# Half-array products of two heads issued in turn in every attention of a three-layer network

## The chip, the cores and the metric

One core of a Trainium2 chip runs the whole program. The metric is the device time of one execution in microseconds (us), the median of three. Between kernels, a difference of less than about 0.2% (3.7 us) can't be told from no change.

## What is computed

One sequence of 256 tokens, 1024 wide, goes through one block of a first kind and two layers of a second kind, all in float32. The parts that the change touches are the attentions:

```python
# first block: forgetting attention, 8 heads of 64, causal
sc = einsum('bqhd,bkhd->bhqk', qb, k) * scale + decay;  p = softmax(where(dist >= 0, sc, -inf))
o  = einsum('bhqk,bkhd->bqhd', p, v)
# first block: differential attention, 4 heads, two score maps (c = 0, 1) of 64 each, one value of 128
sc = einsum('bqhcd,bkhcd->bchqk', qb, k) * scale + bias;  w = p[:, 0] - lam * p[:, 1]
# both layers: window attention, 16 query heads of 64 on 4 key heads, |i - j| <= 128
# both layers: dilated attention, 12 sub-heads of 64 in 3 groups (dilation 1, 4, 16), 4 slots,
#              the groups of a slot mixed by their softmax denominators
```

Around them stand dense projections, a gated recurrence and a feed-forward part in the first block, and an expert-choice layer of 16 experts in each of the two layers, whose weights are most of the 562 MB that the program reads.

## The kernel before, in words

Activations stand transposed: features on the 128 partitions, the 256 tokens along the free axis. A dense product (`mm3`, lines 160 to 162) splits weight and activation into a high and a low part and issues three products of 128x128 by 256 columns. Weights come from memory through a ring of three 1 MB tiles, and ScalarE and VectorE split each (lines 154 and 155).

An attention head has 64 features, so two heads (or the two maps of a differential head), c = 0 and c = 1, share 128 partitions. Their **score products** take 64 rows of TensorE's array each (printed 64\*128 in the profile), their **value products** 64 columns each (128\*64), so each is a half-array product. They are plain float32, which the profile shows as two passes of each product.

- `scores` (line 405) is used by the forgetting and the differential attention: per pair of heads a 256-column and a 128-column product for each c.
- Line 460: value products of the forgetting attention, two per head.
- Line 877: value products of the window attention, two of 256 columns per head, eight pairs of heads in each layer. The first reads what ScalarE copied from the transposes of c = 0 (line 289), the second what it copied for c = 1.
- Lines 895 to 936: the dilated attention, written head by head. For each pair j, head c and query tile t there is one bank of scores: 256 columns by full-array products (lines 802 and 803), then two half-array products of 128 columns (line 908). VectorE reads the bank (line 910). After both query tiles of both heads come the value products, all of c = 0 and then all of c = 1 (lines 926 and 932).

Score tiles `ps_s` have two PSUM banks, value and transpose tiles `ps_v` and `ps_t` three together. The code isn't the order of issue: the framework plans it from its own timeline of each engine and fills TensorE with dense products of the projections while an attention waits for the other engines. Each engine then runs its own list strictly in that order, and waits on semaphores. The transposes (`to_T`, line 288) go between scores and values.

After a layer's attentions follow its gates, branch and output projections, and then the experts, whose weights (`we`) are loaded ahead into whatever buffers are free, paced by the projections (`Experts.pace`, `prefetch`).

Of the kernel before, what the change touches and what calls it, by code (L numbers as in the profile page):

```python
# [10 lines left out]
F32 = mybir.dt.float32  # L11
# [69 lines left out]
def tile_net(ctx: ExitStack, tc: tile.TileContext, a, out):  # L81
# [43 lines left out]

    def cols(t, c, n):
        return t[:, c : c + n]

    def pairs(ps):
        return ps.rearrange("p (n t) -> p n t", n=2)  # L130
# [176 lines left out]
    def first_block():  # L307
        with ExitStack() as es:
# [12 lines left out]
            def pss():  # L321
                return pp.tile([P, 512], F32, name="ps_s", tag="s", bufs=2)
# [73 lines left out]
            with tc.tile_pool(name="b1t", bufs=2, side="right", reuse_waits="tile") as tp:  # L396
# [2 lines left out]

                def scores(qs, ks, kt):  # L400
                    pq = [pss(), pss()]
                    for qr, kr, o in ((slice(128, 256), slice(0, 256), 0), (slice(0, 128), slice(0, 128), 256)):
                        for c in range(2):
                            b = slice(64 * c, 64 * c + 64)
                            nc.tensor.matmul(  # L405
                                pq[c][:, o : o + kr.stop], qs[b, kt, qr], ks[b, kt, kr], start=True, stop=True
                            )
                    return pq
# [20 lines left out]
                for j in range(4):  # L429
                    z = tp.tile([P, 2, 384], F32, name="z", tag="z")  # L430
                    pq = scores(fq, fk, j)

                    cm = tp.tile([P, 2, 384], F32, name="cm", tag="cm")
                    o = nck_d[2 * j : 2 * j + 2]
                    for lo, n in ((0, 256), (256, 128)):
                        nc.sync.dma_start(
                            cm[:, :, lo : lo + n],
                            bass.AP(tensor=o.tensor, offset=o.offset, ap=[[0, P], [T, 2], [1, n]]),
                        )
                    for c in range(2):  # L440
                        ends = cm[:, c, 128:384].rearrange("p (b k) -> p b k", b=2)
                        nc.gpsimd.tensor_tensor(
                            ends, ends, one("cmask").unsqueeze(1).to_broadcast([P, 2, P]), op=ALU.add
                        )
                        nc.vector.scalar_tensor_tensor(
                            z[:, c, :], pq[c][:, :384], 0.125, cm[:, c], op0=ALU.mult, op1=ALU.add
                        )
                    rs = soft(z)
                    pts = []
                    for c in range(2):  # L450
                        for t, s in SEG:
                            nc.vector.tensor_scalar(z[:, c, s], z[:, c, s], rs[:, t, c : c + 1], None, op0=ALU.mult)
                        pt = tp.tile([P, 384], F32, name="pt", tag="pt")
                        to_T(blocks(z[:, c]), pp, pt)
                        pts.append(pt)
                    po = psv()
                    for k, qr, pr in ((0, slice(0, 256), slice(0, 256)), (1, slice(128, 256), slice(256, 384))):
                        for c in range(2):
                            hv = slice((2 * j + c) * 64, (2 * j + c) * 64 + 64)
                            nc.tensor.matmul(  # L460
                                po[64 * c : 64 * c + 64, qr], fv[:, k, hv], pts[c][:, pr], start=k == 0, stop=k == 1
                            )
                    split_act(Y[:, 0, 12 + j], Y[:, 1, 12 + j], po[:, :T])
# [260 lines left out]
    def mixer(l, h, stats, w0=None):  # L724

        with ExitStack() as es:
# [107 lines left out]
            for j, pair in enumerate(WIN_PAIRS):  # L834
# [30 lines left out]
                for c in range(2):  # L865
                    for t in range(2):
                        i = 2 * c + t
                        (nc.gpsimd if t == 1 else nc.vector).tensor_scalar(
                            zf[:, i, :], zf[:, i, :], sm[:, i : i + 1], 0.0, op0=ALU.mult, op1=ALU.add
                        )  # L870
                    pt = tp.tile([P, 512], F32, name="pt", tag="pt", bufs=3)
                    to_T([zf[:, 2 * c + t, k * P : k * P + P] for k in range(2) for t in range(2)], pp, pt)
                    pts.append(pt)
                for k in range(2):
                    for c in range(2):
                        kvh = pair[c] // 4
                        nc.tensor.matmul(  # L877
                            po[64 * c : 64 * c + 64, :T], vw[:, k, kvh * 64 : kvh * 64 + 64],
                            pts[c][:, k * T : k * T + T], start=k == 0, stop=k == 1,
                        )  # L880
# [10 lines left out]
            qk(ka, 10, 2)  # L891
            vv(va, 12, 3)
            for j in range(2):
                pts = []
                for c in range(2):
                    s = 2 * j + c
                    b = slice(64 * c, 64 * c + 64)
                    pt = tp.tile([P, 2, 4, P], F32, name="pd", tag="zw")
                    pts.append(pt)
                    for t in range(2):  # L900
                        tk = slice(t * P, t * P + P)
                        z = tp.tile([P, 512], F32, name="zd", tag="pt", bufs=3)
                        ps = pss()
                        parts = ((s, slice(0, T), slice(0, T)), (4 + s, slice(256, 384), tk), (8 + s, slice(384, 512), tk))
                        score(ps[:, :T], qa0[:, j, c, tk], ka0[:, j, c], kl0[:, j, c])
                        for n, o, kr in parts[1:]:
                            i = n // 2 - 2
                            nc.tensor.matmul(ps[:, o], qa[b, i, tk], ka[b, i, kr], start=True, stop=True)  # L908
                        for n, o, kr in parts:
                            nc.vector.scalar_tensor_tensor(  # L910
                                z[:, o], far[:, 1 + t, o], -8.0 * DIL_SLOPES[n], ps[:, o], op0=ALU.mult, op1=ALU.add
                            )
# [6 lines left out]
                        nc.vector.tensor_scalar(z, z, sm, None, op0=ALU.mult)  # L919
                        to_T([z[:, i * P : i * P + P] for i in range(4)], pp, pt[:, t].rearrange("p i q -> p (i q)"))  # L920
                po = psv()
                for c in range(2):
                    s = 2 * j + c
                    o = po[64 * c : 64 * c + 64, :]
                    for k in range(2):
                        nc.tensor.matmul(  # L926
                            o[:, :T], va[:, k, s * 64 : s * 64 + 64], pts[c][:, :, k, :], start=k == 0, stop=False
                        )
                    for i in range(2):
                        n = 4 + 4 * i + s  # L930
                        for t in range(2):
                            nc.tensor.matmul(  # L932
                                o[:, t * P : t * P + P], va[:, t, n * 64 : n * 64 + 64], pts[c][:, t, 2 + i, :],
                                start=False, stop=i + t == 2,
                            )
                split_act(Y[:, 0, j], Y[:, 1, j], po[:, :T])

# [546 lines left out]
```

## Time and profile before

| | |
|---|---|
| median of 3 runs | 1871.66 us (1871.11 to 1874.06) |
| the profiled execution | 1869.36 us, its span 1867.5 us |
| TensorE busy | 1545.2 us (83%) |
| VectorE, ScalarE, GpSimd busy | 824.0, 627.9, 35.3 us |
| read from memory | 558.70 MB |
| first block | 0 to about 507 us |
| attentions of the first layer, of the second | 537 to 656 us, 1216 to 1336 us |
| experts of the first layer, of the second | 749 to 1172 us, 1429 to 1867 us |

The profiled execution is 2.3 us below the median. Times inside the program are counted from the start of the span. Ends of matrix products are modelled, so their starts are what is to be read: what a group costs is the time from its first start to the next group's start.

### The profile page before, as it was taken

The page shows a single profiled execution, that of the slowest core. Times are in us where ns is not written, and L with a number is a line of the kernel's source. Part 1 is how long each engine was busy: PE and PEld are TensorE (multiplying, and loading weights), DVE is VectorE, ACT ScalarE, POOL GpSimd, SP SyncE. Part 2 cuts the span into 40 slices and gives each one's busy share as a digit, 9 for nine tenths or more (in the row PEclk, how much of TensorE's full clock was granted, in tenths as well). Part 3 has the DMA queues.
Part 4 walks back from the last instruction along what each step waited for, and adds up shares of the span by engine and source line. Part 5 has one row for each costly group of instructions (what it writes and reads, how often), then busy time and mean ns, then how long its engine had stood idle before and what let it go on. Part 6 is the DMA issues. An engine that isn't in the chain of part 4 may idle for free.

```text
span 1867.5 us, 27365 instructions
## 1 busy us (share of the span) xinstructions
PE 1545.2 (83%) x11458; PEld 1089.8 (58%) x11458; DVE 824.0 (44%) x1479; ACT 627.9 (34%) x1128; POOL 35.3 (2%) x60
## 2 busy tenths in 40 slices
PE   8999999999999999776666656899998766656665
PEld 7899999999998899220211101898996211101111
DVE  7678777997588656210010001687564110000001
ACT  5467646666566544000000000566443100000001
POOL 0100000000011000000000000011000000000000
PEclk9999999999999999887777877999999987878778
DMA  6454455555572378899999999943488999999997
GB/s 249 147 198 161 161 203 180 182 181 181 187 282 92 122 284 338 353 425 426 423 426 424 424 427 423 354 165 109 158 337 304 421 426 426 425 425 425 424 425 320
DMA packets 66260, 562.33 MB, mean 301 GB/s; under 512 B 7500, under 2 KB 12632, under 8 KB 14936
## 3 DMA queue, kind: packets, MB, share of 16 engines
q1 hardware_dynamic: 65976, 560.05, 75.1%
q8 instruction: 90, 1.47, 0.3%
q10 hardware_dynamic: 160, 0.52, 0.1%
q14 instruction: 34, 0.28, 0.0%
HBM read 558.70 MB, written 1.85 MB: 300 GB/s over the span
## 4 chain that ended last, share of the span: by engine, by line
PE 53%; DMA 44%; DVE 2%; ACT 0%; issue 0%; SPq 0%; POOL 0%; ACTq 0%; DVEq 0%
DMA we<-in_w_exp_dram 43%; PE ps_d L160 14%; PE ps_d L162 14%; PE ps_d L161 14%; PE ps_t L288 2%; PE ps_v L877 1%; PE ps_g L1190 1%; PE ps_s L802 1%; PE ps_s L908 1%; PE ps_u L1190 1%; PE ps_s L803 1%; PE ps_t L1205 0%; PE ps_s L405 0%; PE ps_v L926 0%; PE ps_v L932 0%
## 5 line engine op out<-in xcount | busy, mean ns | idle before, releaser
L160 PE MATMUL ps_d<-H,ws 128*128 128x256 f32 x1408 | 403.6, 287 | 8.9 <-ACT H L208 7.7
L162 PE MATMUL ps_d<-H,ws 128*128 128x256 f32 x1408 | 403.4, 287 | 0.9 <-DVE ws L155 0.8
L161 PE MATMUL ps_d<-H,ws 128*128 128x256 f32 x1408 | 402.2, 286 | 0.3 <-DVE H L209 0.3
L155 DVE TENSOR_TENSOR ws<-w,ws 128x1024 fp32r<-128x1024 f32 x282 | 344.1, 1222 | 120.6 <-ACT ws L154 117.3
L154 ACT CAST ws<-w 128x1024 fp32r<-128x1024 f32 x282 | 293.8, 1046 | 262.1 <-PE ps_d L162 235.9
L160 PEld LDWEIGHTS ps_d<-H,ws 128*128 128x128 f32 x1408 | 272.0, 193 | 12.3 <-ACT H L208 7.6
L162 PEld LDWEIGHTS ps_d<-H,ws 128*128 128x128 f32 x1408 | 271.9, 193 | 3.6 <-issue 1.5
L161 PEld LDWEIGHTS ps_d<-H,ws 128*128 128x128 f32 x1408 | 272.0, 193 | 2.3 <-issue 0.8
L1190 PE MATMUL ps_u<-we,W 128*32 128x512 f32 x992 | 168.7, 806 | 107.8 <-DMA we<-in_w_exp_dram 107.8
L1190 PE MATMUL ps_g<-we,W 128*32 128x512 f32 x1024 | 159.0, 734 | 74.5 <-DMA we<-in_w_exp_dram 73.8
L1190 PE MATMUL ps_e<-we,W 128*32 128x512 f32 (+1 forms) x1152 | 155.1, 661 | 73.6 <-DMA we<-in_w_exp_dram 73.6
L1190 PEld LDWEIGHTS ps_u<-we,W 128*32 128x32 f32 x992 | 30.6, 129 | 236.3 <-DMA we<-in_w_exp_dram 185.0
L1190 PEld LDWEIGHTS ps_g<-we,W 128*32 128x32 f32 x1024 | 28.8, 121 | 186.3 <-DMA we<-in_w_exp_dram 133.1
L1264 ACT ACTIVATE W<-ps_g 128x512 f32<-128x512 f32 x16 | 9.6, 597 | 379.9 <-PE ps_g L1190 379.9
L1190 PEld LDWEIGHTS ps_e<-we,W 128*32 128x32 f32 x1152 | 33.1, 121 | 173.9 <-DMA we<-in_w_exp_dram 125.8
L1266 DVE SCALAR_TENSOR_TENSOR W<-W,ps_u 128x512 f32<-128x512 f32 x16 | 11.0, 687 | 244.9 <-PE ps_u L1190 244.9
L1219 DVE COPY W<-ps_e 128x512 f32<-128x512 f32 (+1 forms) x18 | 11.4, 633 | 225.5 <-PE ps_e L1190 225.5
L1271 ACT COPY W<-ps_t 128x512 f32<-128x512 f32 x16 | 9.4, 586 | 266.6 <-PE ps_t L1270 266.6
L1265 DVE SCALAR_TENSOR_TENSOR W<-W,ps_g 128x512 f32<-128x512 f32 x16 | 11.0, 688 | 197.6 <-ACT W L1264 197.6
L160 PE MATMUL ps_d<-Y,ws 128*128 128x256 f32 x288 | 80.8, 281 | 0.0
L161 PE MATMUL ps_d<-Y,ws 128*128 128x256 f32 x288 | 80.7, 280 | 0.0
L162 PE MATMUL ps_d<-Y,ws 128*128 128x256 f32 x288 | 80.7, 280 | 0.0
(321 smaller groups left out, 2349.1 us busy)
## 6 DMA issues: line engine op xcount, KB each, us to landing
we<-in_w_exp_dram SPq DMA_DIRECT2D x122, 2048.0 KB, 29.5
we<-in_w_exp_dram SPq DMA_DIRECT2D x134, 1024.0 KB, 24.7
w<-in_w_in_dram SPq DMA_DIRECT2D x46, 1024.0 KB, 4.9
w<-in_w_up_dram SPq DMA_DIRECT2D x22, 1024.0 KB, 4.8
w<-in_w_br_dram SPq DMA_DIRECT2D x18, 1024.0 KB, 5.0
w<-in_w_gate_dram SPq DMA_DIRECT2D x12, 1024.0 KB, 4.9
w<-in_w_out_dram SPq DMA_DIRECT2D x12, 1024.0 KB, 4.8
w<-in_w_down_dram SPq DMA_DIRECT2D x11, 1024.0 KB, 4.8
```

Of the source, the lines that this page charges most:

```text
L154: nc.scalar.copy(ws[:, 0], s)
L155: nc.vector.tensor_tensor(ws[:, 1], s, ws[:, 0].bitcast(F32), op=ALU.subtract)
L160: nc.tensor.matmul(ps, wh, xh, start=first, stop=False)
L161: nc.tensor.matmul(ps, wh, xl, start=False, stop=False)
L162: nc.tensor.matmul(ps, wl, xh, start=False, stop=last)
L288: nc.tensor.transpose(ps[:, i * P : i * P + P], b, ident)
L802: nc.tensor.matmul(ps, q, kh, start=True, stop=False)
L803: nc.tensor.matmul(ps, q, kl, start=False, stop=True)
L877: nc.tensor.matmul(po[64 * c : 64 * c + 64, :T], vw[:, k, kvh * 64 : kvh * 64 + 64], pts[c][:, k * T : k * T + T], start=k == 0, stop=k == 1,)
L908: nc.tensor.matmul(ps[:, o], qa[b, i, tk], ka[b, i, kr], start=True, stop=True)
L1190: nc.tensor.matmul(b[32 * e : 32 * e + 32, :cn], lhs[:, k, 32 * e : 32 * e + 32], cols(w, ((k - k0) * 4 + e) * cn, cn), start=k == 0, stop ...
L1219: nc.vector.tensor_copy(ye[:, s], E[:, :cn])
```

## The change

A helper issues each half-array product of a group after the one that it issued before, so that the planner can't put the second ahead of the first; and every loop over the two heads, now the inner one, runs c = 1 first and then c = 0. In the dilated attention the loop over query tiles is outermost: both heads' banks of scores are made together, then VectorE works on both, and the value products of the two heads alternate.

```diff
+    def in_a_row():
+        last = [None]
+        def matmul(*args, **how):
+            with tc.issue_after(last[0].ins) if last[0] else nullcontext():
+                last[0] = nc.tensor.matmul(*args, **how)
+        return matmul
...
                 def scores(qs, ks, kt):
                     pq = [pss(), pss()]
+                    matmul = in_a_row()
...
-                        for c in range(2):
+                        for c in (1, 0):
...
-                            nc.tensor.matmul(
+                            matmul(
                                 pq[c][:, o : o + kr.stop], qs[b, kt, qr], ks[b, kt, kr], start=True, stop=True
...
+                matmul = in_a_row()
                 for k in range(2):
-                    for c in range(2):
+                    for c in (1, 0):
                         kvh = pair[c] // 4
-                        nc.tensor.matmul(
+                        matmul(
                             po[64 * c : 64 * c + 64, :T], vw[:, k, kvh * 64 : kvh * 64 + 64],
...
-                for c in range(2):
-                    s = 2 * j + c
...
-                    for t in range(2):
-                        tk = slice(t * P, t * P + P)
...
-                        ps = pss()
...
-                            nc.tensor.matmul(ps[:, o], qa[b, i, tk], ka[b, i, kr], start=True, stop=True)
+                for t in range(2):
+                    tk = slice(t * P, t * P + P)
+                    pq = [pss(), pss()]
+                    for c in range(2):
+                        score(pq[c][:, :T], qa0[:, j, c, tk], ka0[:, j, c], kl0[:, j, c])
+                    matmul = in_a_row()
+                    for i in range(2):
+                        for c in (1, 0):
+                            matmul(
+                                pq[c][:, 256 + P * i : 384 + P * i], qa[HALF[c], 2 * i + j, tk],
+                                ka[HALF[c], 2 * i + j, tk], start=True, stop=True,
+                            )
...
-                for c in range(2):
-                    s = 2 * j + c
-                    o = po[64 * c : 64 * c + 64, :]
-                    for k in range(2):
...
+                for k in range(2):
+                    for c in (1, 0):
+                        s = 2 * j + c
+                        matmul(
...
+                for i in range(2):
+                    for t in range(2):
+                        for c in (1, 0):
```

The forgetting attention's value products (line 460) are changed like those of the window attention. How the planned order moves is seen at three places, all on TensorE. In the changed kernel the half-array products carry the helper's line, L136; dense products are L171 to L173, transposes L299, full-array scores L815 and L816. A product is one row here, though it has two passes in the profile.

Window attention, first layer, the value products of a pair, before:

```order
L161 MATMUL ps_d<-H,ws 128x256
L162 MATMUL ps_d<-H,ws 128x256
L877 MATMUL ps_v<-pt,Q 64x256
L288 MATMUL ps_t<-cv,zw 128x128 x2
L877 MATMUL ps_v<-pt,Q 64x256 x3
L288 MATMUL ps_t<-cv,zw 128x128 x6
L802 MATMUL ps_s<-kh,qw 128x256
```

The same pair in the changed kernel:

```order
L173 MATMUL ps_d<-H,ws 128x256
L171 MATMUL ps_d<-H,ws 128x256
L136 MATMUL ps_v<-pt,Q 64x256 x4
L299 MATMUL ps_t<-cv,zw 128x128 x8
L815 MATMUL ps_s<-kh,qw 128x256
```

The lone product ahead of the transposes has joined the other three. In all 16 pairs of both layers it stands alone before, with transposes, dense products or scores behind it, and in all 16 the four stand together after; 28 dense products stand between the pair's transposes and its value products here, where 24 stood before.

Dilated attention, first layer, last scores and first values, before:

```order
L802 MATMUL ps_s<-ka_6720,qa_6719 128x256
L803 MATMUL ps_s<-kl_6721,qa_6719 128x256
L908 MATMUL ps_s<-Q 128x128
L288 MATMUL ps_t<-cv,zd 128x128 x4
L926 MATMUL ps_v<-pd,Q 64x256 x2
L932 MATMUL ps_v<-pd,Q 64x128 x4
L908 MATMUL ps_s<-Q 128x128
L802 MATMUL ps_s<-ka_6720,qa_6719 128x256
L803 MATMUL ps_s<-kl_6721,qa_6719 128x256
L908 MATMUL ps_s<-Q 128x128 x2
```

And in the changed kernel:

```order
L815 MATMUL ps_s<-ka_6720,qa_6719 128x256
L816 MATMUL ps_s<-kl_6721,qa_6719 128x256
L136 MATMUL ps_s<-Q 128x128 x4
L136 MATMUL ps_v<-pd,Q 64x256 x4
L136 MATMUL ps_v<-pd,Q 64x128 x8
L299 MATMUL ps_t<-cv,zd 128x128 x4
```

Eight groups of two half-array scores in a layer (two of them cut in two, as here) have become four groups of four, and four groups of six value products two groups of twelve, none cut. The score tiles' two banks are both taken by one query tile; between a group and the first product that needs one of its banks again stand 27 or more products. The last group of values of a layer, 57 products ahead of the first branch product before, has moved behind the first six of them; 14 products stand between the last transposes and it.

Differential attention, scores of the second head, before:

```order
L161 MATMUL ps_d<-H,ws 128x256
L405 MATMUL ps_s<-Qb,Qa 128x256
L405 MATMUL ps_s<-Qb,Qa 128x128
L405 MATMUL ps_s<-Qb,Qa 128x256
L405 MATMUL ps_s<-Qb,Qa 128x128
L162 MATMUL ps_d<-H,ws 128x256
```

And in the changed kernel:

```order
L136 MATMUL ps_s<-Qb,Qa 128x256
L171 MATMUL ps_d<-H,ws 128x256
L172 MATMUL ps_d<-H,ws 128x256
L173 MATMUL ps_d<-H,ws 128x256
L136 MATMUL ps_s<-Qb,Qa 128x256
L136 MATMUL ps_s<-Qb,Qa 128x128 x2
L171 MATMUL ps_d<-H,ws 128x256
```

Here a whole group has been cut: each product waits for the bank that it writes, and the planner fills the time between the two banks with dense products. Of the eight score groups of the first block, five are whole before and three cut in halves of two; in the changed kernel three are whole and five cut behind the first product, one of these once more. No instruction of GpSimd has moved; on SyncE's list one load of experts' weights in each layer stands one weight load later.

## Rows read from the trace of the kernel before

**Rows 1.** The page, part 4: the chain that ended last, by engine.

```profile
PE 53%; DMA 44%; DVE 2%; ACT 0%; issue 0%; SPq 0%; POOL 0%; ACTq 0%; DVEq 0%
```

**Rows 2.** Stretches: length, busy us of PE, PEld, DVE, ACT, POOL; PEclk, DMA share, GB/s.

```profile
537.00:603.00 66.00, 66.00 (x517) 60.00 (x516) 55.89 (x104) 43.14 (x105) 10.82 (x12) 1.00 0.36 131
603.00:656.00 53.00, 53.00 (x377) 44.40 (x376) 32.88 (x83) 29.55 (x61) 2.15 (x5) 1.00 0.35 128
749.00:1172.00 423.00, 281.07 (x1798) 78.53 (x1798) 35.58 (x64) 20.75 (x48) 0.00 (x0) 0.80 0.99 417
750.00:755.00 5.00, 3.53 (x15) 1.53 (x15) 1.73 (x5) 0.27 (x1) 0.00 (x0) 0.50 0.03 13
```

**Rows 3.** Timeline of PE, window attention: start us, us, instructions (one per pass).

```profile
559.52 0.28 PE L162 MATMUL ps_d<-H,ws 128*128 128x256 f32 x1
559.73 0.65 PE L877 MATMUL ps_v<-pt,Q 128*64 128x256 f32 x2
560.31 0.44 PE L288 MATMUL ps_t<-cv,zw 128*128 128x128 f32 x2
560.67 1.08 PE L877 MATMUL ps_v<-pt,Q 128*64 128x256 f32 x6
561.68 0.87 PE L288 MATMUL ps_t<-cv,zw 128*128 128x128 f32 x6
562.31 0.36 PE L802 MATMUL ps_s<-kh,qw 128*128 128x256 f32 x1
```

**Rows 4.** Timeline of PE, forgetting attention, the one pair whose values stand together.

```profile
78.22 0.87 PE L460 MATMUL ps_v<-pt,Qa 128*64 128x256 f32 x8
79.02 0.39 PE L160 MATMUL ps_d<-H,ws 128*128 128x256 f32 x1
```

**Rows 5.** Timeline of PE, differential attention: scores of one head whole, of another cut.

```profile
104.09 0.92 PE L405 MATMUL ps_s<-Qb,Qa 64*128 64x256 f32 x8
...
114.20 0.92 PE L405 MATMUL ps_s<-Qb,Qa 64*128 64x256 f32 x4
115.05 0.39 PE L161 MATMUL ps_d<-H,ws 128*128 128x256 f32 x1
```

**Rows 6.** Timeline of PE, dilated attention: values of one head, twelve passes.

```profile
640.02 0.28 PE L162 MATMUL ps_d<-H,ws 128*128 128x256 f32 x1
640.23 1.08 PE L926 MATMUL ps_v<-pd,Q 128*64 128x256 f32 x4
...
642.11 0.66 PE L288 MATMUL ps_t<-cv,zd 128*128 128x128 f32 x4
```

**Rows 7.** Timeline of PE, dilated attention: a group of scores whole, half of one cut.

```profile
603.18 0.71 PE L908 MATMUL ps_s<-Q 64*128 64x128 f32 x4
603.82 0.39 PE L802 MATMUL ps_s<-ka,qa 128*128 128x256 f32 x1
604.04 0.28 PE L803 MATMUL ps_s<-kl,qa 128*128 128x256 f32 x1
...
637.47 0.48 PE L908 MATMUL ps_s<-Q 64*128 64x128 f32 x2
637.89 0.39 PE L802 MATMUL ps_s<-ka,qa 128*128 128x256 f32 x1
```

**Rows 8.** Timeline of PE, forgetting attention: the one long wait; in brackets idle time, releaser.

```profile
60.33 1.23 PE L405 MATMUL ps_s<-Qa 64*128 64x256 f32 x4 [3.06 <-DVE z L445]
...
61.87 0.41 PE L161 MATMUL ps_d<-H,ws 128*128 128x256 f32 x1
62.08 0.41 PE L162 MATMUL ps_d<-H,ws 128*128 128x256 f32 x1
```

**Rows 9.** Groups by line and shape, 603 to 656 us: busy us, mean ns | idle before.

```profile
L289 ACT COPY pd<-ps_t 128x512 f32<-128x512 f32 x8 | 4.7, 586 | 3.7 <-PE ps_t L288 3.5
...
L910 DVE SCALAR_TENSOR_TENSOR zd<-far,ps_s 128x128 f32<-128x128 f32 x16 | 3.8, 280 | 0.0
L910 DVE SCALAR_TENSOR_TENSOR zd<-far,ps_s 128x256 f32<-128x256 f32 x8 | 3.3, 419 | 3.6 <-PE ps_s L908 2.7 <-PE ps_t L288 0.8
```

More of the change, by code (lines that the diff above doesn't have):

```diff
@@ L873, in mixer @@
                     pts.append(pt)
+                matmul = in_a_row()
                 for k in range(2):
-                    for c in range(2):
+                    for c in (1, 0):
                         kvh = pair[c] // 4
-                        nc.tensor.matmul(
+                        matmul(
                             po[64 * c : 64 * c + 64, :T], vw[:, k, kvh * 64 : kvh * 64 + 64],
@@ L893, in mixer @@
             for j in range(2):
-                pts = []
-                for c in range(2):
-                    s = 2 * j + c
-                    b = slice(64 * c, 64 * c + 64)
-                    pt = tp.tile([P, 2, 4, P], F32, name="pd", tag="zw")
-                    pts.append(pt)
-                    for t in range(2):
-                        tk = slice(t * P, t * P + P)
-                        z = tp.tile([P, 512], F32, name="zd", tag="pt", bufs=3)
-                        ps = pss()
[L904 to L907, printed above, removed]
-                            nc.tensor.matmul(ps[:, o], qa[b, i, tk], ka[b, i, kr], start=True, stop=True)
-                        for n, o, kr in parts:
+                pts = [tp.tile([P, 2, 4, P], F32, name="pd", tag="zw") for _ in range(2)]
+                for t in range(2):
[3 more added lines that the diff above has]
+                        score(pq[c][:, :T], qa0[:, j, c, tk], ka0[:, j, c], kl0[:, j, c])
+                    matmul = in_a_row()
+                    for i in range(2):
[4 more added lines that the diff above has]
+                            )
+                    for c in range(2):
+                        s, ps, pt = 2 * j + c, pq[c], pts[c]
+                        z = tp.tile([P, 512], F32, name="zd", tag="pt", bufs=3)
+                        for n, o in ((s, slice(0, T)), (4 + s, slice(256, 384)), (8 + s, slice(384, 512))):
                             nc.vector.scalar_tensor_tensor(
@@ L921, in mixer @@
                 po = psv()
-                for c in range(2):
-                    s = 2 * j + c
-                    o = po[64 * c : 64 * c + 64, :]
-                    for k in range(2):
-                        nc.tensor.matmul(
-                            o[:, :T], va[:, k, s * 64 : s * 64 + 64], pts[c][:, :, k, :], start=k == 0, stop=False
-                        )
[L929 to L934, printed above, removed]
+                matmul = in_a_row()
+                for k in range(2):
+                    for c in (1, 0):
+                        s = 2 * j + c
+                        matmul(
+                            po[64 * c : 64 * c + 64, :T], va[:, k, s * 64 : s * 64 + 64], pts[c][:, :, k, :],
+                            start=k == 0, stop=False,
+                        )
+                for i in range(2):
+                    for t in range(2):
+                        for c in (1, 0):
+                            n = 4 + 4 * i + 2 * j + c
+                            matmul(
+                                po[64 * c : 64 * c + 64, t * P : t * P + P], va[:, t, n * 64 : n * 64 + 64],
+                                pts[c][:, t, 2 + i, :], start=False, stop=i + t == 2,
                             )
```

## The prediction, made before the changed kernel ran

> **What bounds the kernel now.** I read the chain of work that ended last first [rows 1]: 53% of it is TensorE's, 44% waits for memory. The two belong to different stages. The stretches [rows 2] tell which: in the first layer's attentions, 537 to 656 us, TensorE is busy in every microsecond, at a granted clock of 1.00 (2.4 GHz), while the DMA queues are at 0.35; in the experts, 749 to 1172 us, the queues are at 0.99 and TensorE works 281 of 423 us. The second layer repeats both. The change lies in the attentions, so what it saves on TensorE shortens them as long as TensorE doesn't begin to wait there. Whether the end of the program moves too depends on how the experts' stage starts; row 750 to 755 answers it: the queues move 13 GB/s there, because every buffer that may be filled ahead is full and the first has not yet been used up. The stage begins in that state however early it comes.
>
> **How half-array products run.** The reader is to see three things in the timelines. First, a lone product of 256 columns (two passes) takes 0.58 us from its start to the next start, 559.73 to 560.31 [rows 3]. Second, neighbours on different halves run at the same time: the six passes behind it (c = 1 of the first key block, then c = 0 and c = 1 of the second) take 1.01 us, 560.67 to 561.68. Two products share the first half of that time, and the third has the second half for itself. In the forgetting attention eight passes, four of 256 and four of 128 columns, take 0.80 us [rows 4]; four of 256 one after the other would by the lone product need 1.16 alone. In the scores, eight passes have the same 0.92 us in their row as four [rows 5]. Third, going into half-array work and out of it costs time: a dense product starts 0.12 us after the one before, but the first half-array product 0.21 after (640.02 to 640.23, [rows 6]), and the second product after such a group stands 0.22 from the first instead of 0.12 (603.82 to 604.04, [rows 7]). So a group pays 0.09 and 0.10 beside its own passes.
>
> At this point a page speaks against the change. The Trainium skill, "TensorE: Matmul & The Clock Gate", Part 3, "What overlaps and what doesn't", has weight loads overlap a running product only when the two use different row groups. Value products of two heads use all rows and differ in columns, so by it the second head's weights would wait for the first head's product. The trace disagrees: six value passes in 1.01 us [rows 3] leave no room for that. By the page the sum below would keep the scores alone and come to about 9 us.
>
> **The change, part by part.**
>
> *Window values*, 16 pairs in two layers, each before as in [rows 3] or with dense products or scores in place of the two transposes. Four products and eight transposes take 2.58 us, 559.73 to 562.31. Together, the four should take what the last three take now, 1.01, since the third's idle half is filled by the fourth; the eight transposes, six of which take 0.63 [rows 3], 0.84. That is 1.85: 0.73 saved, 11.7 in all.
>
> *Dilated values*, four groups of two heads (two a layer). One head's twelve passes take 1.88 us, 640.23 to 642.11 [rows 6], strictly one after another, since head follows head. Alternating, the second head's lie beside the first's: 1.88 and one entry of 0.09 go, four times: 7.9.
>
> *Dilated scores*. A group of one head takes 0.64 us [rows 7], with entry and exit 0.83. Of eight in a layer two are cut; a half takes 0.42 (637.47 to 637.89), with entry and exit 0.61, so a cut group 1.22. A layer pays 6 x 0.83 + 2 x 1.22 = 7.4. After, four groups with two heads side by side (as in [rows 5], where eight passes take no longer than four) pay 4 x 0.83 = 3.3. Saved: 4.1 a layer, 8.2.
>
> *Forgetting values*. Three of four pairs stand cut like the window's, the fourth whole [rows 4]; all four are whole after. At the same 0.73: 2.2.
>
> *Scores of the first block* lose. A whole group takes 0.85 (114.20 to 115.05 for half of a cut one, and the whole has the same row [rows 5]); cut in halves 2 x 0.85 + 0.19 = 1.89; cut behind the first product, which the trace doesn't show, some 0.58 for the lone one [rows 3], at most 0.80 for the other three [rows 4], and 0.19: 1.57. Two groups that were whole get cut (+1.44), two go from halves to this form (-0.64), one falls in three pieces (0.58 + 0.80 + 0.42 and two switches, 2.18 for 1.89: +0.3). Together +1.1; its ends are 0 and +2.
>
> *New waits*. A pair's first value product now needs the copy of its second head, one ScalarE copy (0.59 us, [rows 9]) later than before. Were it waited for each time, 24 groups would cost 14 us. But the planner has put it behind more dense products: 28 at 0.12 us are 3.4 us, and two copies take 1.2. If that cover went, TensorE, which runs strictly in its order, would hold up the dense products behind it, and with them the splits of the next weights. For the dilated scores both banks are taken by one query tile, and VectorE needs 2 x (0.42 + 2 x 0.28) = 2.0 us to read both [rows 9]; the 27 products or more ahead of the next use are 3.2 us. Only the last values of a layer have little ahead of them, 14 products (1.7 us) behind their last transposes, and they stand in front of branch products. I put 0.5 us a layer on that, 1.0; the ends are 0 and 4. The long wait of the first block, 3.06 us until VectorE frees a bank [rows 8], stays: the product that is now first takes the bank that comes free first. The load of experts' weights that moves behind a weight load on SyncE's list costs nothing while the queues are at 0.35 [rows 2].
>
> *Sum*: 11.7 + 7.9 + 8.2 + 2.2 - 1.1 - 1.0 = 27.9 us. The profiled execution of 1869.4 us becomes 1841.5; the median shown is 2.3 us above it, so I predict 1843.8.
>
> **Rivals.**
>
> 1. *Value products of two heads don't share the array in the new order.* For it: no row shows one key block's two heads with c = 1 first, and the page above. Against: in [rows 3] a c = 1 product goes ahead of a c = 0 one and the two share. Then the window values save only the interruption, 0.73 - 0.58 = 0.15 each, 2.4; the forgetting ones 0.5; dilated values 0.4; scores 8.2; less 2.1: 9.4 us, 1862.3.
>
> 2. *The gain is waited away in the experts.* For it: 44% of the chain is memory [rows 1], and if the loads ahead depended on time, not on the projections, the experts would begin with fewer buffers filled. Against: row 750 to 755. Left is the first block's 2.2 - 1.1: 1870.6, no measurable change.
>
> 3. *Waits for the score banks, slower.* Place: the dilated scores, where one query tile holds both banks and the next one's first product stands at the head of TensorE's list until VectorE has read them. Price: the one such wait in the trace [rows 8] costs 3.06 us and a slow clock behind it; dense products then start 0.21 apart (61.87 to 62.08) instead of 0.12, at the lower of the two levels; for a dozen of them that is another 1.1. At 4.1 each, eight tiles (four in each of two layers) would cost 33, and the time would be 1877; below seven of the eight the change still gains. Against: 3.2 us of products ahead for 2.0 us of reading.
>
> **How the numbers follow.** A change of under 0.2% (3.7 us) can't be told from none here. Chances: the forecast 0.84, rival 1 0.06, rival 2 0.06, rival 3 0.04. Faster is the forecast and rival 1, 0.90; no change rival 2, 0.06; slower 0.04. The forecast's own range: 3 us more if cut groups and waits cost nothing and switches cost more than I counted, giving 1838 with the spread of the runs; up to 9 us less if waits reach 4, the scores of the first block lose 2 and half of the dilated scores fail to overlap, giving 1853. That holds eight in ten; 1838 to 1853.
>
> **What would show it.** Right: in the changed trace the window's values stand as one row of eight passes whose next start is 1.0 us later; a dilated row of values of both heads ends some 1.9 us after it starts; TensorE stays busy through the attentions, which are 13 to 14 us shorter in each layer; the experts' stage keeps its 423 us and starts 15 and 28 us earlier. Wrong: eight value passes that take near 1.6 us (rival 1), an experts' stage that grows (rival 2), or idle time ahead of dilated scores with a granted clock below 1.00 there (rival 3).

## The result and the profile after

| | before | changed |
|---|---|---|
| median of the runs beside each other | 1871.79 us (4 runs) | 1849.35 us (4 runs, 1843.96 to 1851.8) |
| ratio, 95% interval | | 0.9873, 0.9856 to 0.989 |
| profiled execution, its span | 1869.36, 1867.5 us | 1849.56, 1847.7 us |
| first window score starts | 537.18 | 542.69 |
| layer 1, first window score to first expert product | 215.85 | 202.30 |
| the same, layer 2 | 215.78 | 202.26 |
| experts, first product to next layer's first window score; last stage to the end | 463.74; 434.95 | 464.33; 436.12 |

The time fell by 22.4 us, into the range (1838 to 1853), 5.5 short of the forecast. The gain stands in the two layers, 13.55 and 13.52 us, where the prediction had 13.4 each. The first block, forecast 1.1 us shorter, is 5.5 longer in this profile. The two profiled executions differ by 19.8 us: 27.1 less in the layers, 5.5 more in the first block, 1.8 more in the experts.

The chain of the changed kernel, by engine (compare [rows 1]):

```profile
PE 53%; DMA 44%; DVE 2%; ACT 1%; issue 1%; SPq 0%; POOL 0%; ACTq 0%; DVEq 0%
```

Its stretches, the attentions of layer 1 in two parts and the experts (columns as in [rows 2]):

```profile
542.70:603.00 60.30, 60.30 (x501) 56.98 (x500) 53.07 (x102) 41.32 (x98) 9.54 (x12) 1.00 0.40 142
603.00:651.90 48.90, 48.90 (x424) 45.57 (x423) 37.72 (x88) 34.15 (x71) 2.17 (x5) 1.00 0.38 134
745.00:1168.00 423.00, 281.39 (x1824) 77.54 (x1824) 34.42 (x60) 21.40 (x49) 0.00 (x0) 0.80 1.00 419
```

TensorE is busy in every microsecond of the attentions at a granted clock of 1.00, as before: nothing that was saved came back as a wait there. The experts start 8.0 and 21.0 us earlier and keep their rate: the queues stay full, and the stages differ by 0.6 and 1.2 us.

TensorE's timeline of the changed kernel, at the places of [rows 3], [rows 4], [rows 6] and [rows 7]:

```profile
565.50 0.28 PE L171 MATMUL ps_d<-H,ws 128*128 128x256 f32 x1
565.71 1.08 PE L136 MATMUL ps_v<-pt,Q 128*64 128x256 f32 x8
566.73 1.09 PE L299 MATMUL ps_t<-cv,zw 128*128 128x128 f32 x8
567.58 0.36 PE L815 MATMUL ps_s<-kh,qw 128*128 128x256 f32 x1
...
77.99 0.87 PE L136 MATMUL ps_v<-pt,Qa 128*64 128x256 f32 x8
78.79 0.88 PE L299 MATMUL ps_t<-cv,z 128*128 128x128 f32 x6
...
623.13 0.72 PE L136 MATMUL ps_s<-Q 64*128 64x128 f32 x8
623.78 0.39 PE L171 MATMUL ps_d<-H,ws 128*128 128x256 f32 x1
...
639.61 1.96 PE L136 MATMUL ps_v<-pd,Q 128*64 128x256 f32 x24
641.49 0.66 PE L299 MATMUL ps_t<-cv,zd 128*128 128x128 f32 x4
```

Read starts, not lengths. Eight window passes take 1.02 us (565.71 to 566.73), where six took 1.01 and the lone two 0.58. Eight transposes follow in 0.85. Eight score passes of two dilated heads take 0.65, where four of one head took 0.64; 24 value passes take 1.88, where twelve did. The halves of the array work side by side in all of them.

The last dilated values of layer 1, in the same view; in brackets the idle time ahead and its releaser:

```profile
652.51 0.28 PE L173 MATMUL ps_d<-Y,ws 128*128 128x256 f32 x1
652.72 1.96 PE L136 MATMUL ps_v<-pd,Q 128*64 128x256 f32 x24
655.15 0.50 PE L171 MATMUL ps_d<-Y,ws 128*128 128x256 f32 x2 [0.47 <-ACT Y L198]
```

Here is the new wait of the layers. The value products don't wait. The branch product behind them does, since it reads what ScalarE makes of them (line 198): 0.47 us in each layer.

The first block in the same view: the old wait [rows 8] with what follows it, and a new one.

```profile
60.29 1.18 PE L136 MATMUL ps_s<-Qa 64*128 64x256 f32 x2 [2.61 <-DVE z L457]
61.40 0.58 PE L171 MATMUL ps_d<-H,ws 128*128 128x256 f32 x1
61.78 0.41 PE L172 MATMUL ps_d<-H,ws 128*128 128x256 f32 x1
61.99 0.41 PE L173 MATMUL ps_d<-H,ws 128*128 128x256 f32 x1
...
112.70 0.70 PE L136 MATMUL ps_s<-Qb,Qa 64*128 64x256 f32 x2 [1.09 <-DVE z L531]
```

And VectorE's and SyncE's timelines ahead of the second wait:

```profile
112.09 1.02 DVE L531 SCALAR_TENSOR_TENSOR z<-ps_s,bias 128x384 f32<-128x384 f32 x2 [4.57 <-DMA bias<-scr]
```

```profile
96.49 0.27 SPq L504 DMA_DIRECT2D row_d<-rr  x1
99.09 0.80 SPq L509 DMA_DIRECT2D rows<-row_d  x2
102.55 0.37 SPq L512 DMA_DIRECT2D scr<-rows  x1
...
105.26 2.10 SPq L518 DMA_DIRECT2D bias<-scr  x4
```

The differential scores' bank is read by VectorE only when a chain of transfers (rows stored, loaded on all partitions, stored skewed, loaded as bias) has landed. VectorE stands 4.57 us for it, TensorE 1.09 us for VectorE. One more wait is new in the first block, in the products that spread the norms of the differential heads, which stand there without any idle time in the profile of before:

```profile
173.35 2.02 PE L244 MATMUL ps_v<-cv,orr 128*128 128x128 f32 x16 [0.56 <-DVE orr L557]
```

### The profile page after: what moved, and what is told of

The parts are those of the page before. It is cut to its first block, busy times and chain, and to the rows that moved or that the text cites. A ratio compares the mean times of both kernels' runs of the same rounds, so it can differ in the third digit from the quotient of the medians.

```text
span 1847.7 us, 27346 instructions
## 1 busy us (share of the span) xinstructions
PE 1524.7 (83%) x11458; PEld 1078.8 (58%) x11458; DVE 823.0 (45%) x1479; ACT 630.2 (34%) x1130; POOL 32.6 (2%) x60
## 4 chain that ended last, share of the span: by engine, by line
PE 53%; DMA 44%; DVE 2%; ACT 1%; issue 1%; SPq 0%; POOL 0%; ACTq 0%; DVEq 0%
DMA we<-in_w_exp_dram 40%; PE ps_d L171 14%; PE ps_d L172 14%; PE ps_d L173 14%; PE ps_t L299 1%; PE ps_g L1208 1%; PE ps_v L136 1%; DMA XB<-in_rows_dram 1%; DMA w<-in_w_in_dram 1%; PE ps_u L1208 1%; PE ps_t L1223 1%; PE ps_s L136 1%; PE ps_s L815 1%; PE ps_s L816 1%; DVE ws L166 0%
## 5 line engine op out<-in xcount | busy, mean ns | idle before, releaser
L171 PE MATMUL ps_d<-H,ws 128*128 128x256 f32 x1408 | 403.9, 287 | 9.2 <-ACT H L219 7.9
L173 PE MATMUL ps_d<-H,ws 128*128 128x256 f32 x1408 | 404.0, 287 | 1.2 <-DVE ws L166 1.2
L171 PEld LDWEIGHTS ps_d<-H,ws 128*128 128x128 f32 x1408 | 273.7, 194 | 11.5 <-ACT H L219 7.9
L173 PEld LDWEIGHTS ps_d<-H,ws 128*128 128x128 f32 x1408 | 273.7, 194 | 2.7 <-DVE ws L166 1.6
L1208 PE MATMUL ps_u<-we,W 128*32 128x512 f32 x992 | 164.9, 788 | 109.5 <-DMA we<-in_w_exp_dram 109.5
L1208 PE MATMUL ps_e<-we,W 128*32 128x512 f32 (+1 forms) x1152 | 159.5, 677 | 71.6 <-DMA we<-in_w_exp_dram 71.4
L171 PE MATMUL ps_d<-Y,ws 128*128 128x256 f32 x288 | 80.7, 281 | 0.9 <-ACT Y L198 0.9
L173 PE MATMUL ps_d<-Y,ws 128*128 128x256 f32 x288 | 80.6, 280 | 0.0
```

What stands on the lines that cost most here:

```text
L171: nc.tensor.matmul(ps, wh, xh, start=first, stop=False)
L173: nc.tensor.matmul(ps, wl, xh, start=False, stop=last)
L1208: nc.tensor.matmul(b[32 * e : 32 * e + 32, :cn], lhs[:, k, 32 * e : 32 * e + 32], cols(w, ((k - k0) * 4 + e) * cn, cn), start=k == 0, stop ...
```

## The experiments

My first theory was that the edit makes the first block's loss: a slow clock that lasts longer behind the wait at 60 us, the wait at 112.7, and score groups cut in pieces. The rival was that this loss is the execution's, not the edit's. Then the runs turn to which part of the edit pays in the layers. "Layer" is always first window score to first expert product, of layer 1 and 2; every median stands beside the kernel before on the same chip.

| | layer, us | first window score | median | ratio to before, 95% |
|---|---|---|---|---|
| E1 layers only | 202.32, 202.27 | 540.1 | 1847.08 | 0.986, 0.9843 to 0.9877 |
| E2 first block only | 215.84, 215.70 | 536.8 | 1872.37 | 0.9996, 0.9986 to 1.0007 |
| E3 first scores back | 202.30, 202.25 | 542.3 | 1847.42 | 0.9858, 0.9838 to 0.9877 |
| E4 bias early | 202.30, 202.26 | 539.7 | 1845.87 | 0.9848, 0.9829 to 0.9866 |
| E5 the changed kernel again | 202.30, 202.26 | 537.7 | 1848.39 | 0.9866, 0.9847 to 0.9884 |
| E6 window only | 209.24, 209.20 | 534.9 | 1860.08 | 0.9936, 0.9919 to 0.9953 |
| E7 c = 0 first | 211.08, 210.92 | 541.0 | 1864.39 | 0.9956, 0.9941 to 0.9971 |
| E8 head after head | 204.54, 204.48 | 540.8 | 1850.68 | 0.9882, 0.9864 to 0.9899 |
| E9 dilated only | 209.27, 209.12 | 539.4 | 1858.81 | 0.9934, 0.9913 to 0.9955 |
| E10 untied | 204.85, 204.79 | 541.3 | 1851.13 | 0.9894, 0.9873 to 0.9915 |
| E11 combined | 202.32, 202.25 | 537.6 | 1844.89 | 0.9863, 0.984 to 0.9886 |
| E12 two and two | 201.95, 201.89 | 540.0 | 1843.47 | 0.9851, 0.9831 to 0.987 |

**E1, the layers alone.** Both loops of the first block as before:

```diff
-                    matmul = in_a_row()
-                        for c in (1, 0):
+                        for c in range(2):
-                            matmul(
+                            nc.tensor.matmul(
```

> The layers' attentions as in the changed kernel, the first block as before. Theory: the two layers save 13.5 us each as the two profiles show (first window score to first expert product 215.8 to 202.3), and the 5.5 us that the first block lost don't arise: about 1844.8 us, some 4.5 below the changed kernel. Rival: the first block's loss is not the edit's but the chip's (a clock that stays low by chance behind the wait at 60 us): then about 1849, as the changed kernel, with a first block that still ends 5 us late.

Measured 1847.08. The layers repeat 202.3, and the first block, instruction for instruction that of before on every engine, now begins the window at 540.1 where the profile of before had 537.2. Between the two forecasts, and a first sign that the place of the first block moves without an edit. It isn't the rival's place, though: behind the wait at 60 us the clock is that of before (0.72, then 1.00). Of the 2.9 us, 1.7 arose at the bias (E1's PE timeline), where the profile of before has no wait: 1.16 ahead of the group, which then takes 1.31 instead of 0.85,

```profile
111.73 1.38 PE L416 MATMUL ps_s<-Qb,Qa 64*128 64x256 f32 x8 [1.16 <-DVE z L529]
113.04 0.38 PE L173 MATMUL ps_d<-H,ws 128*128 128x256 f32 x1
```

and 1.5 behind a wait of 2.66 us that both have at 513 to 515 us, by the granted clock (stretches of before and of E1, columns as in [rows 2]):

```profile
508.00:520.00 12.00, 9.34 (x78) 9.13 (x78) 9.58 (x20) 8.52 (x14) 0.57 (x3) 1.00 0.82 314
508.00:520.00 12.00, 9.34 (x65) 9.13 (x66) 8.28 (x18) 8.81 (x14) 0.57 (x3) 0.86 0.73 279
```

**E2, the first block alone.** The window and dilated attention taken from the kernel before, the rest from the changed one.

> The first block's scores and values as in the changed kernel, the layers' attentions as before. Theory: its first window score comes 5.5 us late, as in the changed kernel, and nothing gives it back: about 1877 us. By the prediction's terms (2.2 gained by the values, 1.1 lost by the scores) it would be 1870.7. Rival: the loss is the chip's clock by chance: then within 2 us of 1871.8.

Measured 1872.37, no change, and the theory falls: up to the window attention its lists are those of the changed kernel on every engine, and it stands there at 536.8 instead of 542.7. Stretches 60:66 and 66:72 (columns as in [rows 2]) show where the two part; first the changed kernel, then E2, then E5, the changed kernel once more:

```profile
60.00:66.00 6.00, 5.71 (x21) 4.48 (x21) 4.87 (x9) 1.86 (x8) 1.47 (x3) 0.53 0.54 188
66.00:72.00 6.00, 6.00 (x29) 5.49 (x29) 4.43 (x9) 2.91 (x9) 1.68 (x3) 0.62 0.66 234
```

```profile
60.00:66.00 6.00, 6.00 (x45) 5.29 (x44) 5.52 (x14) 2.80 (x9) 1.23 (x2) 1.00 0.47 142
66.00:72.00 6.00, 6.00 (x46) 5.18 (x46) 5.96 (x12) 4.02 (x12) 3.75 (x4) 1.00 0.54 205
```

```profile
60.00:66.00 6.00, 6.00 (x32) 5.04 (x33) 5.53 (x11) 2.58 (x9) 1.47 (x2) 0.72 0.48 148
66.00:72.00 6.00, 6.00 (x43) 4.78 (x42) 5.60 (x15) 4.07 (x12) 2.14 (x4) 1.00 0.61 228
```

The column behind POOL is the granted clock. The same list of instructions, behind the same wait, ran there at 0.53 and 0.62, at 1.00 throughout, or at 0.72 and then 1.00; TensorE got 50, 91 and 75 instructions done in these 12 us. From the group that waits to the first forgetting values the changed kernel took 17.70 us (60.29 to 77.99), E2 13.17 (59.16 to 72.33), E5 14.69 (59.95 to 74.64).

**E3, the first block's scores back.** Only `scores` as before, the forgetting values changed.

> All of the change but the scores of the first block, which are issued as before. Theory: the scores' order makes the whole loss (the longer stretch of slow clock behind 60 us, the new wait at 112.7, the cut groups), and the values gain what the prediction said, 2.2: about 1842.5 us, the first window score near 535. Rival: tying the forgetting values delays the first block (its value products wait for the second head's copy, and all behind them comes later): then the first window score stays near 542 and the time near 1849.

The window began at 542.3, but E2 forbids reading the place of one profile as the edit's. Inconclusive on its own. It does show the wait for the bias (1.29 us at 112.4) without the scores' new order.

**E4, bias early.** The changed kernel with the rows' product, copy and store moved ahead:

```diff
                 qk(fk, 2)
+                row_d = dp.tile([4, 384], F32, name="row_d", tag="row_d")
...
+                psr = psv()
+                nc.tensor.matmul(psr[:4, :384], one("rel", 33), one("onehot", 33), start=True, stop=True)
...
+                nc.sync.dma_start(row_d, rr)
                 vv(fv, 0)
                 for j in range(4):
```

> The changed kernel, but the small product that makes the relative bias rows, its copy and its store are written ahead of the forgetting heads, so that the chain of bias transfers can begin earlier. Theory: the wait of 1.09 us at 112.7 and the slow clock behind it (28 dense products in 5.04 us instead of 3.3) go: 2.8 us, about 1846.5. Rival: the chain is held by the tiles that it shares with the forgetting heads, or the wait shows up at another place: 1849 as the changed kernel.

Measured 1845.87, as expected. SyncE's and VectorE's timelines of E4:

```profile
94.33 1.75 SPq L518 DMA_DIRECT2D bias<-scr  x4
...
99.36 2.22 SPq L518 DMA_DIRECT2D bias<-scr  x4
```

```profile
105.21 1.02 DVE L531 SCALAR_TENSOR_TENSOR z<-ps_s,bias 128x384 f32<-128x384 f32 x2 [1.30 <-PE ps_s L136]
```

The bias loads leave 11 us earlier, VectorE now waits for the scores and not for them, and TensorE has no idle time there. The clock behind the wait at 60 us was as low as in the changed kernel's own profile (0.56 and 0.59 in the two stretches), so this run gained at the other place: from the group that waits at 60 us to the first window score it took 479.0 us (60.65 to 539.68), the changed kernel's profile 482.4.

**E5, the changed kernel again.**

> The changed kernel itself, once more. New theory, since the first block of the kernel with only the first block changed stood 5.9 us earlier than the same list of products in the changed kernel (first window score 536.8 against 542.7): the place of the first block differs from execution to execution by up to 6 us, by how long the slow clock lasts behind its waits and by whether the bias transfers come late. Then the layers repeat 202.3 us to 0.1, the first window score lies somewhere from 536 to 543, and the median of more runs comes to 1845 to 1849. Rival: the first block's loss belongs to the changed kernel: 542.7 again within 0.5, and 1849.4.

First window score 537.7, layers the same to 0.1, median 1848.39: the new theory holds. In the eight profiles whose first block is that of before, the first window score lies from 534.9 to 541.3, 539.3 in the mean; in the three with the changed one from 536.8 to 542.7, mean 539.1.

**E6, the window values alone, and E9, the dilated attention alone.**

> Only the window attention's value products changed (c = 1 first, tied), the rest as before. Theory: each of 16 pairs saves 0.73 us, so a layer takes 215.8 - 5.8 = 210.0 us from the first window score to the first expert product, and the time falls by 11.7 us to about 1861. Rival: what the dilated attention waited for swallows part of it: above 212.

> Only the dilated attention changed (regrouped, tied, c = 1 first), the window's values and the first block as before. Theory: what the window alone left of the gain is the dilated attention's: with 202.3 us a layer for both and 209.2 for the window alone, 215.8 - 6.9 = 208.9 us a layer, and 13.8 less in all, about 1858. The prediction's terms would make it 8.05 - 0.5 a layer, 208.2. Rival: the two depend on each other: the dilated attention alone gains under 5.

Each gives 6.6 us a layer, together 13.2 of 13.5, so the two add up. The window's part is above my 5.8, since in E6 the dilated scores, whose code is as before, were planned whole too: 16 groups of two products where before had 12 and 8 halves. The dilated part is 1.0 below the 7.55 of the prediction's terms; one of its four score groups is cut in E9's first layer (six passes and two), which costs 0.4 and a switch of 0.19.

**E7, c = 0 first.** `for c in (0, 1)` for `for c in (1, 0)` in the layers, ties kept.

> The layers' attentions regrouped and tied as in the changed kernel, but with c = 0 first and then c = 1; the first block as before. The order of issue then shows all 16 pairs of window values still cut behind the first product, the dilated values cut in 1 and 11, and six of eight groups of dilated scores cut. Theory: wholeness is what pays, not the ties: no gain in the window, and about 3 us a layer from each of the dilated values and scores: near 210 us a layer, 1862 in all. Rival: the ties and the regrouping do the work: 202.3 us a layer, 1847.

Layers of 211, as the theory had it. The window in E7's timeline is cut as before, ties or not:

```profile
563.55 0.65 PE L136 MATMUL ps_v<-pt,Q 128*64 128x256 f32 x2
564.13 0.44 PE L299 MATMUL ps_t<-cv,zw 128*128 128x128 f32 x2
564.50 1.08 PE L136 MATMUL ps_v<-pt,Q 128*64 128x256 f32 x6
565.51 0.87 PE L299 MATMUL ps_t<-cv,zw 128*128 128x128 f32 x6
```

A tie keeps a product from going ahead of the one before it; it doesn't keep the first from going alone. With c = 1 first, the first product is the one that has to wait for the second copy, and the rest can follow at once.

**E8, head after head.**

```diff
-                for k in range(2):
-                    for c in (1, 0):
+                for c in (1, 0):
+                    for k in range(2):
```

and the same in the dilated values: six products of c = 1 and then six of c = 0.

> The layers' attentions as in the changed kernel, groups whole and tied, but the value products of the window and the dilated attention run head after head (all of c = 1, then all of c = 0) instead of in turn; the first block as before. Theory: neighbours share the array only when they use different column halves. Then a window group takes 1.88 us (eight passes at the 0.235 of the dilated row of before) instead of 1.02, and a dilated one about twice what it takes in turn: 6.9 and 3.6 us more a layer, near 212.8 us a layer and 1868 in all. Rival: being whole is enough: 202.3 us a layer, 1847.

Wrong for the window, half right for the dilated attention: eight window passes took 1.02 us, not 1.88, 24 dilated ones 3.23, not 3.76. E8's timeline:

```profile
563.83 1.09 PE L136 MATMUL ps_v<-pt,Q 128*64 128x256 f32 x8
564.85 1.09 PE L299 MATMUL ps_t<-cv,zw 128*128 128x128 f32 x8
...
635.86 3.31 PE L136 MATMUL ps_v<-pd,Q 128*64 128x256 f32 x24
639.09 0.66 PE L299 MATMUL ps_t<-cv,zd 128*128 128x128 f32 x4
```

Pass by pass, the second head's first starts at 637.21, ahead of three passes of the first head (637.32, 637.42 and 637.53) that stand before it in the list. So what was said of the engines ahead of the prediction, that each runs its list strictly in order, doesn't hold between the two column halves: there a pass starts past a few waiting ones.

**E12, two and two.** As E8, but the dilated heads change after every two products.

> As the run with the value products head after head, but in the dilated attention the heads alternate after two products (of two passes each) instead of after one or after six. Theory, formed on that run: the array takes up products of the other half past up to four waiting passes (window groups of two and two ran in 1.02 us, dilated ones of six and six in 3.24): then a dilated group takes 1.9 us as in strict turn, and a layer 202.3. Rival: the window ran together by its size alone, and the dilated group lies between 1.9 and 3.2, near 2.6: 203.7.

E12's timeline:

```profile
563.00 1.09 PE L136 MATMUL ps_v<-pt,Q 128*64 128x256 f32 x8
564.02 1.09 PE L299 MATMUL ps_t<-cv,zw 128*128 128x128 f32 x8
...
635.03 2.01 PE L136 MATMUL ps_v<-pd,Q 128*64 128x256 f32 x24
636.97 0.66 PE L299 MATMUL ps_t<-cv,zd 128*128 128x128 f32 x4
...
648.92 2.01 PE L136 MATMUL ps_v<-pd,Q 128*64 128x256 f32 x24
650.86 0.39 PE L171 MATMUL ps_d<-H,ws 128*128 128x256 f32 x1
```

1.94 us, near the 1.88 of strict turn: products of the other half are taken up while two (four passes) of the first half are left, but in E8 not before that. A layer is 0.4 us shorter than in the changed kernel, because the last values stand ahead of a dense product of `H`, which doesn't need their result: the wait of 0.47 is gone, the 0.05 more of each dilated group paid.

**E10, untied.** `in_a_row` without its `issue_after`.

> The layers' attentions regrouped, c = 1 first, but no product tied to the one ahead of it; the first block as before. In the order of issue the value groups are then whole all the same; only the dilated scores fall apart (12 twos, 2 threes, 2 ones instead of 8 fours). Theory: the order of c makes the value groups whole, and the ties matter for the scores alone: eight groups of fours in two layers become sixteen, at 0.42 + 0.19 for each half against 0.65 + 0.19 for a whole one, 1.5 us more a layer: 203.8 us a layer, 1850. Rival: without ties the values lose too: above 208.

The values stay whole without ties, in the window as here:

```profile
564.29 1.08 PE L135 MATMUL ps_v<-pt,Q 128*64 128x256 f32 x8
```

The scores fall apart, and a layer is 2.5 us longer, not 1.5; the wait of 0.47 is gone here too, so the scores cost about 3.0. E10's timeline shows why: a half group is two products on the same rows, one behind the other, and lasts as long as the whole group of four (0.64, where I had put 0.42):

```profile
622.65 0.71 PE L135 MATMUL ps_s<-Q 64*128 64x128 f32 x4
623.29 0.39 PE L172 MATMUL ps_d<-H,ws 128*128 128x256 f32 x1
```

**E11, combined**: E3 with E4's move.

> The layers' attentions and the forgetting values as in the changed kernel, the first block's scores as before, and the product, copy and store of the bias rows ahead of the forgetting heads, as in the run with the early bias. Theory: with the bias wait gone and fewer cut score groups it is at least as good as the changed kernel with the early bias alone (1845.9): 1844, first window score 535 to 540. Rival: the first block's place is set by the slow clock behind the wait at 60 us alone, and the median is that of the changed kernel, 1849.

1844.89, no bias wait, first window score 537.6. By the ratios it can't be told from E4 (0.9848), and not from the changed kernel either (0.9873 and 0.9866): theory and rival both stand.

## Why the prediction came out as it did

*What bounds it, and the experts.* Right. All that the layers saved reached the end; rival 2 is out. The stages of the experts vary by a microsecond without an edit of the layers (in E2 the last one takes 436.36, in the profile of before 434.95).

*Window values*, 0.73 a pair. Right: 2.58 became 1.87 (565.71 to 567.58), 0.71. Rival 1 is out: the Trainium skill's rule in "TensorE: Matmul & The Clock Gate", Part 3, "What overlaps and what doesn't", by which only weight loads for other row groups overlap, is contradicted by eight passes in 1.02 us on two column halves, all on the same 128 rows: in the changed kernel two weight loads start at 565.98 and 565.99, one for each half, beside the products that start with them; the next products begin at 566.20.

*Dilated values*, 1.97 a group. Right in size: 2 x 1.88 became 1.88.

*Dilated scores*, 4.1 a layer. Right: 0.65 for two heads, with entry and exit 0.84, four times. No wait for their banks, the clock at 1.00: rival 3 is out.

*New waits*, 0.5 a layer for the last values. The size came out, 0.47, but by luck, since the wait is another: the branch product behind them waits for what ScalarE makes of their result, while they themselves don't wait for their operands. That the planner puts other work there at no cost shows in E12.

*Forgetting values and first scores.* Added up from the starts in E6 (the old list) and E2 (the changed one), both granted 1.00 there, the groups' lengths with 0.19 for each entry and exit: the values save 2.3 (predicted 2.2), the scores lose 1.3 (predicted 1.1; a cut behind the first product costs 0.63 + 0.85 + 0.19 - 0.85 = 0.8, I had 0.72).

*The step that failed* is "the long wait of the first block ... stays", taken as a constant, and with it that the first block has no other wait that could open.

First, two waits opened. Each of the three profiles with the changed first block waits about 1 us for the bias (1.09 in the first, E2 and E5 below); of the eight with the old one, E1 alone does. And each of the three waits 0.56 us ahead of line 244, none of the eight.

```profile
106.86 0.70 PE L136 MATMUL ps_s<-Qb,Qa 64*128 64x256 f32 x2 [0.91 <-DVE z L531]
109.24 0.70 PE L136 MATMUL ps_s<-Qb,Qa 64*128 64x256 f32 x2 [0.98 <-DVE z L531]
```

What the edit does to the first block at the fast clock can be read from E2 against E6, both granted 1.00 from 49 to 511 us: from the first score group to the first product behind the wait at 511 us, 462.45 us (48.86 to 511.31) with the changed list and 461.95 (48.95 to 510.90) with the old one. That is 0.5 longer where 1.1 shorter was forecast; the two waits make 1.5 us.

Second, what follows a wait isn't constant. Behind the one at 60 us the low clock cost nothing in E2, 1.5 us in E5 and 4.5 us in the changed kernel's profile, in executions of one list. Behind the bias wait that profile alone of the three was at the lower level (0.72 in 113 to 119 us), some 1.5 us more. Behind the wait of 2.66 us at 511 to 519 us, which all fourteen profiles have, nine were granted the lower level for a while, at about 1.5 us each (E1 above); before and the changed kernel's first profile are not among them. So the profile of before that I forecast from stood 2.1 us early against the mean of its eight likes, the profile after 3.6 late against the mean of its three: most of the 5.5 in the profiles is that.

The 5.5 of the medians is another figure, but it moves at the same places: E5's profiled execution, 1843.49, is 6.1 us shorter than the first one, 1849.56, of the same kernel, and 5.0 of that is the first block. Six of the eight runs of the changed kernel lie at 1848 to 1852. By the ratios, which take in all runs, the saving is 23.8 (0.9873) and 25.1 us (0.9866). Taking the bias wait away (E4) brought the median from 1849.0 (eight runs) to 1845.9; the intervals of the ratios overlap, and E11, also without the wait, has 0.9863 where E4 has 0.9848, so it is not shown that this wait makes what the median lacks.

What stays open: what decides, in one and the same list, whether the clock stays low behind the wait; and how much of what the median lacks is the bias. E12 with the early bias was not run.

## What to carry to other kernels

Half-array products of two heads should be issued as one unbroken group; what makes the group whole is to issue first the product whose operand comes last, and a tie alone doesn't; for the scores it took the tie as well (E10). Price a group by the step from its first start to the next group's start, with its entry and exit. Before an edit of a few microseconds is read off two profiles, run one of the kernels again: a stage with a wait and a slow clock behind it can move by 5 us with no edit at all (542.69 and 537.70), while the layers, at 1.00 throughout their attentions, repeat to 0.1.

## What was not expected of the hardware

- Value products on the other column half start while two products (four passes) of the first half still queue ahead of them: 1.02 us for two and two (E8), 1.94 for twelve products changing after two (E12), 3.23 for six and six (E8). They do so ahead of passes that stand before them in the list (637.21 against 637.32 to 637.53 in E8).
- One list of instructions behind one wait of 2.4 to 3.0 us was granted 0.53, 0.72 or 1.00 in the 6 us from 60 us on, in three executions; the lowest cost 4.5 us more than the highest. Behind one wait of 2.66 us, nine of fourteen profiles got the lower level.
